# Projecting the first half of the even layer's heads from x without its shift, the shift's projection coming from two more columns of ctx's operand

## The chip, the cores and the metric

The kernel runs on one core of a Trainium2 chip. The metric is the device time of one execution in microseconds (us). Three runs of the kernel before gave a median of 1676.35 us (1673.29 to 1677.78).

## What is computed

Two layers of a transformer over x (512 rows of 1024) and a context ctx (256 rows of 1024), all in float32. The change lies at the very start of layer 0, the even layer:

```python
mod = silu_c @ ada_w[l] + ada_b[l]            # c gives x's six vectors
modc = silu_cc @ ada_w[l] + ada_b[l]          # c_ctx gives ctx's six
sh1, sc1, g1, sh2, sc2, g2 = split(mod, 6)    # 1024 each: shift, scale, gate, ...
a  = rmsnorm(h, norm1_g) * (1 + sc1) + sh1    # "modulate"
ac = rmsnorm(hc, norm1_g) * (1 + csc1) + csh1
...
u, v, q, k, vv = split(a @ w_in, ...)         # even_mixer
q, k = apply_rope(q, cos, sin), apply_rope(k, cos, sin)
...
y = concatenate([chunk_mlp(u, v), diff_out(o)]) @ w_out
```

`q` and `k` hold eight heads of 64, that is four pairs; ctx gets a q and a k as well, without rope. A projection is linear, so `(y + sh) @ W` is `y @ W` plus the row `sh @ W`, which is the same for all 512 rows of x.

## The kernel before

**Layout and precision.** Activations lie transposed: 1024 features as `KT` = 8 tiles of 128 partitions, rows along the free axis (`TX` = 512 for x, `TC` = 256 for ctx, `TA` = 768 together). Float32 precision is had by splitting each operand into a high half rounded to fp32r and the low rest: ScalarE casts the high half, VectorE or GpSimd subtracts it (`split`, lines 115 and 116; for a weight, lines 75 and 78 in `unit`). Each product then takes three matmuls, high by high, high by low, low by high (`mm3`, lines 99 to 101).

**Order.** The kernel is written as one program in the order of the mathematics, and a scheduler places each instruction on its engine by priority, which is the place in the program unless `tc.high_priority` raises it. Each engine then works through its list in order. `tc.issue_after(ins)` holds an instruction behind another one. An edit in one place can therefore change the lists far behind it too.

**The entry of `even`.** SyncE's queue loads x. `squares` and `rstd_diag` work out the norm of each row. The two vectors that layer 0 needs first, scale (`j` = 1) and shift (`j` = 0), are 1024 x 1024 products with c. `ada_load` brings a slab of `ada_w` (1 MB, two tiles of 128 rows, 4 buffers). `ada_step` (line 349) multiplies a tile of it, as the moving operand, with a 128x32 operand `cst` that holds silu(c) and silu(c_ctx): four matmuls, each into its own 32 rows of one PSUM tile `pf`. `ada_out` copies the result (line 356), transposes it (line 358) and adds the bias, for scale also the norm's gain (lines 362 and 366). There are two passes, scale first, then shift, and `warm` (line 374) puts matmuls without use between the steps. Between the passes VectorE multiplies the eight `hx` by scale and norm (line 392).

Then follows a loop over two halves of the heads. In each, for every `k`, a weight `qk[half, k]` (128 x 512, 256 KB) is loaded and split, x's operand `axx[k]` is made in the first half (line 455 adds the shift on ScalarE, line 456 makes the low half on VectorE), and `mm3` adds to four accumulators of 128 x 512 that fill both wide PSUM tiles (`pw`). In the middle of the first half come ctx's norm and, by `modulate` (lines 191 to 193), its operand `axc[k]`. The accumulators are copied out (`evacuate`), ctx is projected by the same weights into two single PSUM banks (`pb`), and x's part of q and k gets its rope. The operands of x and ctx are two slices, 512 and 256 columns, of one tile from a ring of 16 (`ax`). Between all these, `ada_some` puts in the steps for the other four vectors (two at a time, slabs of 128 x 2048).

**Behind the entry** come the V projection, the attention of four head pairs (`head`), the u and v projections and their gelu (`gated`, `gelu`), the norm of v (`turn`), the 128 x 128 mixing matmuls (`mix`, lines 649 and 650, on the one PSUM bank `fill`), the product u * v (line 677), and the splitting of all eight tiles into `cat`. The out projection (`project`) multiplies them with `even_out`, cast eight at a time by `slab`. `residual` (line 757) adds the result to the stream. None of these lines is touched by the change.

PSUM has two wide tiles (`pw`, two banks each), three single banks (`pb`) and one for small things (`pf`, `fill`).

Of the kernel before, what the change touches and what calls it, by code (L numbers as in the profile page):

```python
# [26 lines left out]
class Builder:  # L27
# [72 lines left out]
        mm(out, s[0], m[1], start=False, stop=False, **kw)  # L100
        mm(out, s[1], m[0], start=False, stop=stop, **kw)  # L101

    def ax(self):

        return [self.axp.tile([P, TA], F32R, name=self.uid("ax"), tag="ax", bufs=16) for _ in range(2)]
# [206 lines left out]
    def even(self):  # L312
# [24 lines left out]
        def ada_load(j, n, k):  # L337

            m = 2 // n
            t = self.adap.tile([P, m, n * D], F32, name=self.uid("ar"), tag="ar", bufs=4)  # L340
            src = a["ada0"][k * P:(k + m) * P, j * D:(j + n) * D].rearrange("(k p) c -> p k c", p=P)
            self.last_slab = nc.sync.dma_start(t, src)
            return [t[:, i, :] for i in range(m)]

        def ada_step(ps, k, t):

            w = t.shape[-1] // 4
            for q in range(4):
                nc.tensor.matmul(ps[32 * q:32 * q + 32, :w], cst[:, k, :], t[:, w * q:w * q + w], start=k == 0,
                                 stop=k == KT - 1, skip_group_check=True)  # L350

        def ada_out(j, n, ps, pt):

            row = self.tmp("t")
            nb = 2 * n
            nc.scalar.copy(row[:, :nb * P], ps[:, :nb * P])
# [24 lines left out]
        ps0 = self.fill()  # L381
        for k in range(KT):
            ada_step(ps0, k, slabs[k])
            if k % 2:
                slabs += ada_load(0, 1, k - 1)
# [4 lines left out]
        ada_out(1, 1, ps0, scaled)  # L390
        for k in range(KT):
            nc.vector.scalar_tensor_tensor(hx[k], hx[k], self.modcol(0, 1, k, 0), rx, ALU.mult, ALU.mult)
# [12 lines left out]
        loaded, ps_of = [], {}  # L405
# [12 lines left out]
                if k == KT - 1:  # L418
                    ada_out(j, 2, ps_of.pop(j), self.bank())

        hc = []
# [6 lines left out]
        tabs = []  # L428

        def evacuate(ps, n, c, heads):  # L430
            h = heads[n % 2]
# [2 lines left out]
                qk[key] = f3()  # L434
            nc.scalar.mul(qk[key][:, c], ps, 0.125 if n < 2 else 1.0)

        with tc.issue_after(self.last_slab.ins):
            ctx_load()
        for half, heads in enumerate(((0, 1), (2, 3))):
            w2 = [self.wide(), self.wide()]  # L440
            accx = [w[:, h * 512:(h + 1) * 512] for w in w2 for h in range(2)]
            W = []
            for k in range(KT):
                t = self.adap.tile([P, 2, 512], F32R, name=self.uid("wq"), tag="wq", bufs=3) if k % 3 == 2 else None
                with tc.issue_after(self.last_slab.ins) if half == 0 else ExitStack():
                    W.append(self.blocks(a["qk"][half, k], 512, t=t))
                    if half == 0:
                        if k > 4:
                            with tc.issue_after(self.last_w.ins):
                                ada_ahead(1)  # L450
                        if k == 7:
                            tabs += [self.load(self.ropep, a[n], [P, TX], n) for n in ("cos", "sin")]
                if half == 0:
                    t, sh = hx[k], self.modcol(0, 0, k, 0)
                    nc.scalar.activation(axx[k][0], t, AF.Identity, bias=sh)
                    nc.vector.scalar_tensor_tensor(axx[k][1], t, sh, axx[k][0].bitcast(F32), ALU.add, ALU.subtract)  # L456
                elif k % 2:
                    ada_ahead(1)
# [11 lines left out]
            bk = [self.bank() for _ in range(2)]  # L470
            accc = [b[:, h * TC:(h + 1) * TC] for b in bk for h in range(2)]
            for k in range(KT):
                for n in range(4):
                    self.mm3(accc[n], W[k][n], axc[k], k == 0 and n % 2 == 0, k == KT - 1)
                if k % 2 and k > 2 - half:
# [333 lines left out]
    def pair(self, pool):  # L809
        NH = self.T // 2  # L810
        if pool:
            t = pool.tile([P, 2, NH], F32R, name=self.uid("T"), tag="T", bufs=12)
            return t[:, 0, :], t[:, 1, :]
        t = self.axp.tile([P, TA], F32R, name=self.uid("ax"), tag="ax", bufs=16)
        return t[:, :NH], t[:, NH:2 * NH]

    def ffn_rstd(self, half, sq, rest, NH=TA // 2, bank=None):
# [259 lines left out]
    def odd(self):  # L1077
# [133 lines left out]
        raw = {}  # L1211

        def keep(half, n, eng):
            t = self.axp.tile([P, TA], F32R, name=self.uid("ax"), tag="ax", bufs=16)
# [128 lines left out]
```

## Time and profile before

| | |
|---|---|
| median of three runs | 1676.35 us |
| the profiled execution | 1676.23 us, its span 1674.4 us |
| TensorE busy | 1550.9 us (93%) |
| VectorE busy | 1152.9 us (69%) |
| ScalarE busy | 729.3 us (44%) |
| GpSimd busy | 658.4 us (39%) |
| DMA, mean over the span | 97 GB/s, 161.97 MB |

The span is the time from the first to the last recorded instruction. PE is TensorE's matmuls, PEld its weight loads, DVE VectorE, ACT ScalarE, POOL GpSimd, SP the queue of SyncE that issues the DMAs. In rows of the timeline the first two numbers are the start and the length of a group of instructions, both in us; what stands in brackets is the idle time ahead of it and what ended that. `mean` is TensorE's granted clock as a share of full speed. The profile divides the span in 40 slices of 41.9 us; the entry is the first three of them.

```profile
## 2 busy tenths in 40 slices
PE   6999989799889899999999988999986899999996
DVE  4622788855987889777766675665668866775675
DMA  8743000232032333444331112101140332323211
```

TensorE is busy for 9 tenths or more of most slices; the first slice, with 6 tenths, is one of the exceptions, and the eighth, where the out projection begins, is another with 7.

### The profile page before, as it was taken

How to read it: one execution, taken by the hardware profiler on the slowest of the kernel's cores; microseconds unless marked ns; L12 is line 12 of the kernel's file. 1: busy time of each engine (PE TensorE's matmuls, PEld its weight loads, DVE VectorE, ACT ScalarE, POOL GpSimd, SP SyncE). 2: the span in 40 equal slices, each digit the busy share in tenths (PEclk: the TensorE clock that was granted, in tenths of full speed). 3: DMA queues.
4: the chain of work that ended last, by engine and by line, in shares of the span. 5: the costliest groups of instructions: out<-in, count | busy, mean ns of one | idle time of the engine just before them, and what ended most of it. 6: DMA issues, size and time to landing. Idle time of an engine off the chain costs nothing.

```text
span 1674.4 us, 24582 instructions
## 1 busy us (share of the span) xinstructions
PE 1550.9 (93%) x9463; PEld 1358.2 (81%) x9463; DVE 1152.9 (69%) x2097; ACT 729.3 (44%) x1464; POOL 658.4 (39%) x477
## 2 busy tenths in 40 slices
PE   6999989799889899999999988999986899999996
PEld 4776878699689899999999877767776788888886
DVE  4622788855987889777766675665668866775675
ACT  2413676533532333333333334555555444444442
POOL 0463211231563433434343236422116755545562
PEclk9999989999899999999999989999998999999998
DMA  8743000232032333444331112101140332323211
GB/s 311 298 170 145 32 7 1 76 133 82 3 123 93 134 122 121 148 139 147 130 128 38 50 60 74 51 13 43 53 158 1 127 108 81 114 76 109 82 38 51
DMA packets 47957, 161.97 MB, mean 97 GB/s; under 512 B 5472, under 2 KB 9952, under 8 KB 40160
## 3 DMA queue, kind: packets, MB, share of 16 engines
q1 hardware_dynamic: 47696, 160.28, 27.0%
q8 instruction: 74, 1.21, 0.3%
q14 instruction: 43, 0.35, 0.1%
q10 hardware_dynamic: 144, 0.13, 0.0%
HBM read 158.29 MB, written 2.10 MB: 96 GB/s over the span
## 4 chain that ended last, share of the span: by engine, by line
PE 66%; DVE 16%; DMA 6%; issue 4%; ACT 4%; POOL 4%; POOLq 0%; SPq 0%; DVEq 0%; ACTq 0%
PE pw L99 8%; PE pb L99 8%; PE pw L100 7%; PE pb L100 7%; PE pw L101 7%; PE pb L101 7%; DMA raw<-ffn_in 4%; PE pf L99 3%; PE pf L100 2%; PE pf L101 2%; PE pb L1198 2%; PE pb L1192 2%; POOL w L903 2%; DVE t L925 2%; DVE junk L220 2%
## 5 line engine op out<-in xcount | busy, mean ns | idle before, releaser
L903 POOL TENSOR_TENSOR w<-raw,w 128x512 fp32r<-128x512 f32 x126 | 173.6, 1391 | 152.2 <-ACT w L901 146.0
L99 PE MATMUL pw<-ax,w 128*128 128x384 f32 (+2 forms) x640 | 209.0, 330 | 17.2 <-DVE hs L984 5.3
L78 POOL TENSOR_TENSOR w<-raw,w 128x512 fp32r<-128x512 f32 (+1 forms) x84 | 127.1, 1520 | 235.4 <-ACT w L75 213.4
L100 PE MATMUL pw<-ax,w 128*128 128x384 f32 (+2 forms) x640 | 208.1, 325 | 2.7 <-DVE ax L456 1.4
L101 PE MATMUL pw<-ax,w 128*128 128x384 f32 (+2 forms) x640 | 206.2, 325 | 1.3 <-POOL w L903 1.1
L903 POOL TENSOR_TENSOR w<-rawo,w 128x512 fp32r<-128x512 f32 x80 | 122.2, 1527 | 198.4 <-ACT w L901 192.2
L757 DVE SCALAR_TENSOR_TENSOR xT<-pb,mod,xT 128x512 f32<-128x512 f32 (+3 forms) x208 | 144.3, 703 | 48.2 <-PE pb L101 47.8
L99 PE MATMUL pw<-T,w 128*128 128x384 f32 (+1 forms) x504 | 159.0, 318 | 17.1 <-DVE hs L975 7.4
L99 PE MATMUL pb<-hh,w 128*128 128x512 f32 x480 | 166.5, 361 | 7.4 <-ACT hh L115 5.3
L100 PE MATMUL pb<-hh,w 128*128 128x512 f32 x480 | 171.2, 358 | 0.9 <-POOL hh L116 0.9
L101 PE MATMUL pb<-hh,w 128*128 128x512 f32 x480 | 168.8, 358 | 0.5 <-POOL w L903 0.5
L100 PE MATMUL pw<-T,w 128*128 128x384 f32 (+1 forms) x504 | 159.1, 316 | 3.5 <-POOL T L116 1.8
L101 PE MATMUL pw<-T,w 128*128 128x384 f32 (+1 forms) x504 | 158.3, 314 | 0.0
L99 PEld LDWEIGHTS pw<-ax,w 128*128 128x128 f32 x640 | 122.9, 193 | 32.5 <-DVE q L979 8.3
L901 ACT CAST w<-t 128x512 fp32r<-128x512 f32 x120 | 74.4, 621 | 151.3 <-DVE t L925 111.7
L100 PEld LDWEIGHTS pw<-ax,w 128*128 128x128 f32 x640 | 123.5, 193 | 10.1 <-DVE ax L193 2.7
L101 PEld LDWEIGHTS pw<-ax,w 128*128 128x128 f32 x640 | 123.3, 193 | 6.1 <-POOL w L903 2.6
L99 PEld LDWEIGHTS pw<-T,w 128*128 128x128 f32 x504 | 97.3, 194 | 23.6 <-ACT T L115 8.8
L116 POOL TENSOR_TENSOR hh<-hs,hh 128x768 fp32r<-128x768 f32 (+1 forms) x42 | 75.9, 1809 | 85.5 <-ACT hh L115 83.1
L99 PE MATMUL pb<-ax,w 128*128 128x256 f32 (+1 forms) x340 | 105.0, 311 | 3.0 <-ACT w L75 1.6
L903 DVE TENSOR_TENSOR w<-t,w 128x512 fp32r<-128x512 f32 x104 | 89.1, 857 | 24.4 <-ACT w L901 23.4
L99 PEld LDWEIGHTS pb<-hh,w 128*128 128x128 f32 x480 | 90.1, 190 | 18.8 <-ACT hh L115 6.0
(384 smaller groups left out, 4160.2 us busy)
## 6 DMA issues: line engine op xcount, KB each, us to landing
raw<-ffn_in SPq DMA_DIRECT2D x44, 1024.0 KB, 4.9
ar<-ada SPq DMA_DIRECT2D x24, 1024.0 KB, 6.7
ar<-ada SPq DMA_DIRECT2D x48, 512.0 KB, 3.5
rawo<-ffn_out SPq DMA_DIRECT2D x44, 512.0 KB, 3.6
raw<-odd_out SPq DMA_DIRECT2D x32, 256.0 KB, 2.6
raw<-qk SPq DMA_DIRECT2D x16, 256.0 KB, 7.7
raw<-uv SPq DMA_DIRECT2D x16, 256.0 KB, 2.7
raw<-even_out SPq DMA_DIRECT2D x8, 512.0 KB, 4.4
```

Source lines behind the costliest of these rows:

```text
L78: eng.tensor_tensor(lo, raw, hi.bitcast(F32), ALU.subtract)
L99: mm(out, s[0], m[0], start=start, stop=False, **kw)
L100: mm(out, s[0], m[1], start=False, stop=False, **kw)
L101: mm(out, s[1], m[0], start=False, stop=stop, **kw)
L116: return (lo_eng or nc.vector).tensor_tensor(lo, src, hi.bitcast(F32), ALU.subtract)
L220: self.nc.vector.scalar_tensor_tensor(junk, t, 1.0, self.cb[who], ALU.mult, ALU.mult, accum_out=self.acc[who][:, col:col + 1])
L757: self.nc.vector.scalar_tensor_tensor(h, ps[:, r], self.modcol(l, j, m, who), h, ALU.mult, ALU.add)
L901: nc.scalar.copy(t[:, 0, :], src)
L903: (eng or nc.gpsimd).tensor_tensor(t[:, 1, :], src, t[:, 0, :].bitcast(F32), ALU.subtract)
L925: nc.vector.tensor_tensor(t, x, y, how)
L1192: nc.tensor.transpose(pt[:, x * P:(x + 1) * P], es[2 * (x % 2) + x // 2][:, kb * P:(kb + 1) * P], self.ident)
L1198: nc.tensor.matmul(po[64 * h:64 * h + 64, :], V[vb][:, 64 * g:64 * g + 64], t[:, h * TC:h * TC + TC], start=kb == 0, stop=kb == nb - 1, sk ...
```

## The change

The pass for the shift no longer stands ahead of the first projection. The second `ada_load`, its eight steps and its 30 warm matmuls go; six warm matmuls stay behind the first pass. Line 392's scaling of `hx` moves into the loop of the first half, and its result is split as it is, without shift, by `split` (lines 118 and 119 now). After that loop `late` issues the shift's slabs, ctx and the rope tables behind the last weight, and a block with the priority of `k` = 2 makes ctx's norm, the eight steps for the shift, its transposes, and ctx's operand. `shift_parts` writes the shift, split in two, in two new columns behind ctx's 256 (tiles of 770 instead of 768 columns). The ctx projection of the first half works on 258 columns, in one wide tile and two banks; its column 256 is `sh @ W`, copied to a 128x1 `b` (line 500) and added to x's part of q or k (line 502). For the second half, and for the V, u and v projections behind it, x's operand is made anew with the shift (`shifted`, lines 429 and 430).

```diff
-        for k in range(KT):
-            nc.vector.scalar_tensor_tensor(hx[k], hx[k], self.modcol(0, 1, k, 0), rx, ALU.mult, ALU.mult)
-        ps0 = self.fill()
-        for k in range(KT):
-            ada_step(ps0, k, slabs[KT + k])
-            warm(slabs[KT + k][:, :P], 3)
-        row = ada_out(0, 1, ps0, scaled)
+        row = ada_out(1, 1, ps0, scaled)
         warm(row[:, :P], 6)
...
-        AX_ = [self.ax() for _ in range(KT)]
+        AX_ = [self.ax(2) for _ in range(KT)]
...
+        def shifted(out, t, sh):
+            nc.scalar.activation(out[0], t, AF.Identity, bias=sh)
+            nc.vector.scalar_tensor_tensor(out[1], t, sh, out[0].bitcast(F32), ALU.add, ALU.subtract)
+
+        def late():
+            with tc.issue_after(self.last_w.ins):
+                sl = sum([ada_load(0, 1, k) for k in range(0, KT, 2)], [])
+                ctx_load()
+            with tc.issue_after(self.last_slab.ins):
+                tabs.extend(self.load(self.ropep, a[n], [P, TX], n) for n in ("cos", "sin"))
+            return sl
+
+        def shift_parts():
+            for k in range(KT):
+                sh = self.modcol(0, 0, k, 0)
+                hi, lo = [t[:, TA:TA + 2] for t in AX_[k]]
+                nc.vector.tensor_copy(hi, sh.to_broadcast([P, 2]))
+                nc.vector.tensor_tensor(lo, sh.to_broadcast([P, 2]), hi.bitcast(F32), ALU.subtract)
...
                 if half == 0:
-                    t, sh = hx[k], self.modcol(0, 0, k, 0)
-                    nc.scalar.activation(axx[k][0], t, AF.Identity, bias=sh)
-                    nc.vector.scalar_tensor_tensor(axx[k][1], t, sh, axx[k][0].bitcast(F32), ALU.add, ALU.subtract)
-                elif k % 2:
-                    ada_ahead(1)
-                    ada_some()
+                    t = hx[k]
+                    nc.vector.scalar_tensor_tensor(t, t, self.modcol(0, 1, k, 0), rx, ALU.mult, ALU.mult)
+                    self.split(*axx[k], t)
+                else:
+                    shifted(axx[k], hx[k], self.modcol(0, 0, k, 0))
+                    if k % 2:
+                        ada_ahead(1)
+                        ada_some()
                 for n in range(4):
                     self.mm3(accx[n], W[k][n], axx[k], k == 0, k == KT - 1)
-                if half == 0 and k == 4:
+                if half == 0 and k == 2:
+                    here = tc.cur_priority
+            if half == 0:
+                sl = late()
+                with tc.high_priority(offset=tc.cur_priority - here):
                     rd = self.rstd_diag([(self.squares(hc, TC), TC)], 1.0 / D)[0]
-                if half == 0 and k == 5:
+                    ps0 = self.fill()
+                    for k in range(KT):
+                        ada_step(ps0, k, sl[k])
+                    ada_out(0, 1, ps0, scaled)
                     rc = self.spread(rd)
+                    shift_parts()
                     for i in range(KT):
                         self.modulate(hc[i], TC, self.modcol(0, 1, i, 1), self.modcol(0, 0, i, 1), rc, axc[i])
...
             for n in range(4):
-                evacuate(accc[n], n, slice(TX, TA), heads)
+                evacuate(bk[n][:, :TC], n, slice(TX, TA), heads)
+                if half == 0:
+                    b = self.small(1, "qb", 4)
+                    nc.scalar.mul(b, bk[n][:, TC:TC + 1], 0.125 if n < 2 else 1.0)
+                    q = qk[n if n < 2 else 2 + n][:, :TX]
+                    nc.scalar.activation(q, q, AF.Identity, bias=b)
```

The lists of the engines below show what the scheduler makes of it. Each row names the line, the operation, its output and inputs, the shape, and how often it stands in a row; the line numbers of the changed kernel are larger (349 is 352 there, 149 is 152, 115 is 118, 205 is 208, 622 is 645, 649 is 672).

VectorE at the entry, before: behind the scaling of `hx` (line 392) come ctx's squares (line 185) and the shift's bias (line 362), then the first low half of x (line 456).

```order
L392 SCALAR_TENSOR_TENSOR hx_5_93<-hx_5_93,mod_66,pb_190 128x512 x2
L392 SCALAR_TENSOR_TENSOR hx_6_95<-hx_6_95,mod_66,pb_190 128x512 x2
L185 TENSOR_TENSOR sq_425<-sq_425,q_427 128x256
L185 TENSOR_TENSOR sq_425<-sq_425,t_430 128x256
L362 TENSOR_TENSOR mod_66<-pb_222,adab_135 128x8
L362 TENSOR_TENSOR mod_67<-pb_222,adab_135 128x8
L185 TENSOR_TENSOR sq_425<-sq_425,q_433 128x256
L185 TENSOR_TENSOR sq_425<-sq_425,t_436 128x256
L185 TENSOR_TENSOR sq_425<-sq_425,q_439 128x256
L456 SCALAR_TENSOR_TENSOR ax_309<-hx_3_89,mod_66,ax_308 128x512
```

The same place after; `subg` is a 128x1 constant of the attention.

```order
L457 SCALAR_TENSOR_TENSOR hx_3_89<-hx_3_89,mod_66,pb_186 128x512 x2
L457 SCALAR_TENSOR_TENSOR hx_4_91<-hx_4_91,mod_66,pb_186 128x512 x2
L457 SCALAR_TENSOR_TENSOR hx_5_93<-hx_5_93,mod_66,pb_186 128x512 x2
L457 SCALAR_TENSOR_TENSOR hx_6_95<-hx_6_95,mod_66,pb_186 128x512 x2
L538 TENSOR_SCALAR subg_1332<-subg_1332 128x1
L119 TENSOR_TENSOR ax_230<-hx_3_89,ax_229 128x512
L119 TENSOR_TENSOR ax_232<-hx_3_89,ax_231 128x512
L119 TENSOR_TENSOR ax_234<-hx_4_91,ax_233 128x512
```

All eight scalings still stand together ahead of the first low half, although the program now has them one by one in the loop; the ctx squares and the shift's bias come later.

ScalarE at the entry, after; `raw` is a weight as loaded, `pf_163` the scale's product.

```order
L75 CAST w_249<-raw_247 128x512
L75 CAST w_269<-raw_267 128x512
L359 COPY t_215<-pf_163 128x256
L75 CAST wq_287<-raw_288 128x512
L75 CAST w_309<-raw_307 128x512
L75 CAST w_329<-raw_327 128x512
L118 CAST ax_229<-hx_3_89 128x512
L75 CAST wq_347<-raw_348 128x512
```

Two weights are cast ahead of the copy of the scale's product, the others behind it.

TensorE at the entry, before: the shift's steps (`ar` is a slab) alternate with warm matmuls, ahead of the first projection.

```order
L358 MATMUL pb_222<-ident_97,t_223 128x128 x2
L349 MATMUL pf_239<-ar_174,cst 32x256 x4
L374 MATMUL pw_103<-ar_174,ones 128x128 x3
L349 MATMUL pf_239<-ar_174,cst 32x256 x4
L374 MATMUL pw_103<-ar_174,ones 128x128 x3
L349 MATMUL pf_239<-ar_188,cst 32x256 x4
```

After, they stand between the projections of the fifth and the seventh of the first half's eight weights (`pw` from `ax` and `wq`, here the sixth):

```order
L352 MATMUL pf_466<-ar_409,cst 32x256 x4
L99 MATMUL pw_245<-ax_239,wq_347 128x512
L352 MATMUL pf_466<-ar_409,cst 32x256
L100 MATMUL pw_245<-ax_240,wq_347 128x512
L352 MATMUL pf_466<-ar_409,cst 32x256
L152 MATMUL pb_447<-ones,sq_423 128x128 x2
L352 MATMUL pf_466<-ar_409,cst 32x256
L101 MATMUL pw_245<-ax_239,wq_347 128x512
L352 MATMUL pf_466<-ar_409,cst 32x256
L99 MATMUL pw_245<-ax_239,wq_347 128x512
L352 MATMUL pf_466<-ar_411,cst 32x256
L100 MATMUL pw_245<-ax_240,wq_347 128x512
```

A step's four matmuls no longer stand in a row there: matmuls of the projection stand between them one at a time.

TensorE where the out projection begins, before: `f` is v's normed tile, `w_3256` the first weight of `even_out`, line 175 the last norm of the attention.

```order
L649 MATMUL pf_3129<-sguT_1295,f_353_1910 128x128 x4
L649 MATMUL pf_3139<-sguT_1295,f_353_1910 128x128 x2
L649 MATMUL pf_3145<-sguT_1295,f_360_1973 128x128 x4
L99 MATMUL pw_3312<-ax_3193,w_3256 128x384
L100 MATMUL pw_3312<-ax_3194,w_3256 128x384
L99 MATMUL pw_3313<-ax_3193,w_3256 128x384
L100 MATMUL pw_3313<-ax_3194,w_3256 128x384
L175 MATMUL pb_2769<-q_2761,ones 128x512
```

After:

```order
L672 MATMUL pf_3166<-sguT_1316,f_365_1994 128x128 x4
L178 MATMUL pb_2790<-q_2782,ones 128x512
L178 MATMUL pb_2793<-q_2787,ones 128x256
L672 MATMUL pf_3176<-sguT_1316,f_365_1994 128x128 x2
L672 MATMUL pf_3182<-sguT_1316,f_372_2057 128x128 x4
L672 MATMUL pf_3192<-sguT_1316,f_372_2057 128x128 x2
L672 MATMUL pf_3198<-sguT_1316,f_379_2120 128x128 x4
L672 MATMUL pf_3208<-sguT_1316,f_379_2120 128x128 x2
L99 MATMUL pw_3333<-ax_3214,w_3277 128x384
```

All mixing now stands ahead of the first matmul of the projection.

ScalarE at the same place, before; `cb` are the copies of c that the next stage needs, `f_554` a tile of u * v.

```order
L622 ACTIVATE f_581_3062<-f_581_3062 128x768
L75 CAST w_3256<-raw_3257 128x1024
L75 CAST w_3255<-raw_3261 128x1024
L115 CAST ax_3207<-f_554_2807 128x768
L205 ACT_TABLE_LOAD
L205 ACTIVATE cb_3265<-cb_3265 128x1024
```

After:

```order
L208 ACTIVATE cb_3289<-cb_3289 128x1024
L118 CAST ax_3228<-f_559_2828 128x768
L118 CAST ax_3234<-f_568_2913 128x768
L118 CAST ax_3240<-f_577_2998 128x768
L118 CAST ax_3246<-f_586_3083 128x768
L118 CAST ax_3250<-o_2477 128x768
L75 CAST w_3277<-raw_3278 128x1024
L75 CAST w_3276<-raw_3282 128x1024
```

The first weights of the out projection are now cast behind the four products and the last tile of the attention.

More of the change, by code (lines that the diff above doesn't have):

```diff
@@ L101, in mm3, with ax, ax_tile @@
         mm(out, s[1], m[0], start=False, stop=stop, **kw)
-    def ax(self):
-        return [self.axp.tile([P, TA], F32R, name=self.uid("ax"), tag="ax", bufs=16) for _ in range(2)]
+    def ax(self, extra=0):
+        return [self.ax_tile()[:, :TA + extra] for _ in range(2)]
+    def ax_tile(self):
+        return self.axp.tile([P, TA + 2], F32R, name=self.uid("ax"), tag="ax", bufs=16)
     def small(self, cols, tag="sm", bufs=6):
@@ L383, in even @@
             ada_step(ps0, k, slabs[k])
-            if k % 2:
-                slabs += ada_load(0, 1, k - 1)
             if k == 3:
@@ L419, in ada_some @@
                     ada_out(j, 2, ps_of.pop(j), self.bank())
-        hc = []
+        hc, tabs = [], []
         def ctx_load():
@@ L426, in ctx_load @@
                 hc.extend(t[:, n, :] for n in range(4))
-        tabs = []
         def evacuate(ps, n, c, heads):
@@ L469, in even @@
                 evacuate(accx[n], n, slice(0, TX), heads)
-            bk = [self.bank() for _ in range(2)]
-            accc = [b[:, h * TC:(h + 1) * TC] for b in bk for h in range(2)]
+            if half == 0:
+                extra = 2
+                w = self.wide()
+                bk = [w[:, :TC + 2], w[:, TX:TX + TC + 2]] + [self.bank()[:, :TC + 2] for _ in range(2)]
+            else:
+                extra = 0
+                bk = [b[:, h * TC:(h + 1) * TC] for b in [self.bank() for _ in range(2)] for h in range(2)]
             for k in range(KT):
                 for n in range(4):
-                    self.mm3(accc[n], W[k][n], axc[k], k == 0 and n % 2 == 0, k == KT - 1)
-                if k % 2 and k > 2 - half:
+                    self.mm3(bk[n], W[k][n], [t[:, TX:TA + extra] for t in AX_[k]], k == 0 and (half == 0 or n % 2 == 0),
+                             k == KT - 1)
+                if k % 2 and (half or k > 3):
                     ada_ahead(1)
@@ L478, in even @@
             for n in range(4):
-                evacuate(accc[n], n, slice(TX, TA), heads)
+                evacuate(bk[n][:, :TC], n, slice(TX, TA), heads)
+                if half == 0:
+                    b = self.small(1, "qb", 4)
+                    nc.scalar.mul(b, bk[n][:, TC:TC + 1], 0.125 if n < 2 else 1.0)
+                    q = qk[n if n < 2 else 2 + n][:, :TX]
+                    nc.scalar.activation(q, q, AF.Identity, bias=b)
             for h in heads:
@@ L813, in pair @@
             return t[:, 0, :], t[:, 1, :]
-        t = self.axp.tile([P, TA], F32R, name=self.uid("ax"), tag="ax", bufs=16)
+        t = self.ax_tile()
         return t[:, :NH], t[:, NH:2 * NH]
@@ L1213, in keep @@
         def keep(half, n, eng):
-            t = self.axp.tile([P, TA], F32R, name=self.uid("ax"), tag="ax", bufs=16)
+            t = self.ax_tile()
             t = t[:, :TC], t[:, TC:TX]
```

9 lines of the change are left out of this document (removed).

## The prediction

> **What bounds it now.** Times below are microseconds from the start of the profiled execution. I read the windows first, then TensorE's timeline, then VectorE, GpSimd and the DMA issues around each of TensorE's gaps. Columns of the windows: length, busy time of PE, PEld, DVE, ACT, POOL, granted clock, DMA share, GB/s.
>
> ```profile
> span 1674.4 us, 24582 instructions
> 40.16:61.19 21.03, 19.36 (x81) 13.84 (x82) 14.68 (x21) 8.17 (x15) 11.46 (x8) 1.00 0.90 331
> 61.19:123.27 62.08, 62.08 (x396) 47.81 (x394) 24.26 (x50) 20.86 (x42) 37.29 (x27) 1.00 0.53 189
> 200.00:300.00 100.00, 88.00 (x546) 76.82 (x547) 85.87 (x218) 69.34 (x144) 12.32 (x8) 0.95 0.01 4
> 320.00:340.00 20.00, 12.12 (x70) 10.72 (x69) 19.06 (x43) 8.81 (x11) 8.73 (x4) 0.74 0.42 133
> 340.00:373.00 33.00, 33.00 (x200) 32.90 (x199) 14.11 (x14) 10.54 (x12) 16.31 (x6) 1.00 0.31 109
> ```
>
> From 61.19 to 123.27 TensorE has no gap (62.08 of 62.08): in the entry every microsecond that work is added to TensorE, or that it starts later, is a microsecond of the kernel. From 320 to 340 it is idle for 7.9 us behind VectorE (19.06 of 20 busy); then it is full again. DMA moves 1 to 4% between 200 and 300, so no backlog of transfers waits there that a delay could hide under. The two places that the change reorders are thus worth their own time.
>
> **The entry: when does TensorE start?** Before, the first projection matmul stands at 40.16, behind the second pass over `ada`:
>
> ```profile
> 25.84 0.37 ACT L356 COPY t<-pf 128x256 f32<-128x256 f32 x1 [15.45 <-PE pf L349]
> 27.14 5.36 DVE L392 SCALAR_TENSOR_TENSOR hx<-hx,mod,pb 128x512 f32<-128x512 f32 x8
> 40.16 0.73 PE L99 MATMUL pw<-ax,w 128*128 128x512 f32 x2 [0.42 <-ACT ax L455]
> ar<-ada SPq DMA_DIRECT2D x1, 1024.0 KB, 14.3
> 46.34 1.07 DVE L128 TENSOR_SCALAR sm<-sm 128x2 int32<-128x2 int32 x1
> 47.32 1.87 DVE L456 SCALAR_TENSOR_TENSOR ax<-hx,mod,ax 128x512 fp32r<-128x512 f32 x1
> 50.48 0.74 DVE L456 SCALAR_TENSOR_TENSOR ax<-hx,mod,ax 128x512 fp32r<-128x512 f32 x1
> 47.34 1.30 POOL L78 TENSOR_TENSOR wq<-raw,wq 128x512 fp32r<-128x512 f32 x1
> 48.61 1.74 POOL L78 TENSOR_TENSOR w<-raw,w 128x512 fp32r<-128x512 f32 x1
> L757 DVE SCALAR_TENSOR_TENSOR xT<-pb,mod,xT x208: 337/740/752, 375.5 to 1658.8; 128x512 f32<-128x512 f32 x88, 128x256 f32<-128x256 f32 x12, 128x384 f32<-128x384 f32 x2, 128x128 f32<-128x128 f32 x2
> ```
>
> The last slab of the first pass is issued at 5.4 and takes 14.3, so it lands at 19.7; the weights now queue right behind it and no longer bind. ScalarE's order puts the third weight's cast behind the copy that ends at 26.2, so GpSimd gets weights three to eight from 26.8 on: six at 1.30 end at 34.6. VectorE meanwhile scales all eight `hx` first: these read one operand from PSUM, and of 208 such operations beside a working GpSimd none took over 752 ns, so 27.14 + 5.36 = 32.5 stands. Then come `subg` and the low half of x, with both operands in SBUF, and these do wait: L128, tiny, lasts 1.07 to the end of a GpSimd operation, and the L456 right behind it loses 1.87 to the next one (0.74 alone). So `subg` waits for the GpSimd operation that ends at 33.3, the first low half for the one that ends at 34.6, and is there at **35.2**. TensorE has run two matmuls by then and stands. Bounds: 33.9 if only one such wait is met, 36 if GpSimd is slowed as in its 1.74. The Trainium skill's "SBUF — State Buffer" (the box of ports) says that whichever of the two starts first holds the shared ports for its whole instruction and the other fully blocks. By that alone VectorE could go first after the one wait, and the start and the sum would be 1.0 lower; the pair L128, L456 lost two turns in a row, so I keep 35.2.
>
> TensorE has then stood for 6 us. What that does to its speed, and what the moved `ada` matmuls cost:
>
> ```profile
> 11.91 2.05 PE L149 MATMUL pb<-ones,sq 128*128 128x128 f32 x8 [11.91 <-DVE sq L185]
> 18.22 0.64 PE L349 MATMUL pf<-ar,cst 128*32 128x256 f32 x8
> 18.79 0.71 PE L374 MATMUL pw<-ar,ones 128*128 128x128 f32 x4
> 1302.09 0.58 PE L99 MATMUL pw<-ax,w 128*128 128x256 f32 x1 [3.17 <-ACT hs L968]
> 1302.46 0.41 PE L100 MATMUL pw<-ax,w 128*128 128x256 f32 x1
> 1305.14 0.28 PE L101 MATMUL pw<-ax,w 128*128 128x256 f32 x1
> 51.92 0.40 PE L99 MATMUL pw<-ax,w 128*128 128x512 f32 x1
> 52.24 1.05 PE L349 MATMUL pf<-ar,cst 128*32 128x512 f32 x4
> 53.23 0.50 PE L100 MATMUL pw<-ax,w 128*128 128x512 f32 x1
> 53.57 0.40 PE L101 MATMUL pw<-ax,w 128*128 128x512 f32 x1
> 53.81 0.40 PE L99 MATMUL pw<-ax,w 128*128 128x512 f32 x1
> 90.66 1.06 PE L349 MATMUL pf<-ar,cst 128*32 128x512 f32 x8
> 62.17 3.63 PE L349 MATMUL pf<-ar,cst 128*32 128x512 f32 x28
> 66.07 0.27 PE L100 MATMUL pb<-ax,w 128*128 128x256 f32 x1
> 62.87 0.88 DVE L193 SCALAR_TENSOR_TENSOR ax<-t,mod,ax 128x256 fp32r<-128x256 f32 x2 [0.18 <-ACT ax L192]
> ```
>
> After 3.17 us of waiting the matmuls run slow from 1302.09 until 1305; at the very start they are slow from 11.91 to 18.22. Half of that is lost: 1.4 to 3.1; I take 2.0. The Trainium skill's "TensorE: Matmul & The Clock Gate" (Part 1) gives about 3.4 us of half rate after an idle window, so 1.7.
>
> The `ada` step costs by group, not by matmul. Two matmuls of 512 columns between projections (x4, two records each) hold TensorE from 52.24 to 53.23; four (x8, at 90.66) last the same 1.06; fourteen in one run take 3.63, four rounds of 0.9. Around a group 0.09 is lost ahead and 0.11 behind (53.23 to 53.57 is 0.34, a matmul 0.23). Four of 256 columns take 18.22 to 18.79 = 0.57. One alone among projections I therefore price at half of 0.9, 0.43, plus the 0.33 of changing over and back: 0.76; bounds 0.14 (a fourth of 0.57, nothing for changing) and 1.0 (the 512 row). In the new order 14 of the 32 stand alone and the others in runs of 5, 6 and 7, two rounds each, 1.2: 14 x 0.76 + 3 x 1.2 = **14.2**. Before, all 32 lay ahead of 40.16. Their cover, `ada` slabs still landing, is gone.
>
> Sum for the entry, at the point where the second half's ctx projection ends (123.27 before):
> - start 35.2 instead of 40.16: -5.0
> - waits of before between 40.16 and 61.19 not repeated (21.03, less 72 matmuls at 0.228, one step of 1.2 and statistics of 0.5): -2.9
> - two matmuls run ahead: -0.5
> - slow TensorE: +2.0
> - `ada` matmuls: +14.2; the two transposes of their result: +0.7
> - ctx: its low halves wait behind VectorE's rewriting of the second half's x. From the shift columns on, 16 tiny operations (2 us), then eight L456 of 0.74 and the L191 and L193 (0.44) mixed among them; the first is hidden by the 16 later `ada` matmuls (3.75), the second comes 1.7 late: +1.7 (0 to 3.5)
> - 512-column `ada` steps in fewer groups: -1.2; two columns on 96 matmuls of 0.12: +0.1
>
> That is **+9.1** (lowest terms -3.5, or +6 with the small matmuls at 0.6; highest +15). The biases (eight short ScalarE operations) and the wide PSUM tile that ctx takes cost nothing: twenty matmuls of the second half stand ahead of the first one that needs that tile. The warm matmuls removed were waiting time. SP's moved loads (slabs, ctx, tables) have 20 us to land.
>
> **The out projection.** The new order also changes what stands at 320 to 373, though no line there is touched:
>
> ```profile
> 325.62 1.80 DVE L128 TENSOR_SCALAR sm<-sm 128x6 int32<-128x6 int32 x1
> 329.11 4.64 POOL L78 TENSOR_TENSOR w<-raw,w 128x1024 fp32r<-128x1024 f32 x2
> 333.70 0.68 DVE L650 TENSOR_TENSOR f<-pf,sgub 128x512 f32<-128x512 f32 x1
> 327.10 1.98 ACT L75 CAST w<-raw 128x1024 fp32r<-128x1024 f32 x2
> 334.43 1.22 PE L649 MATMUL pf<-sguT,f 128*128 128x128 f32 x4 [6.91 <-DVE f L650]
> 336.17 2.08 PE L649 MATMUL pf<-sguT,f 128*128 128x128 f32 x8 [0.52 <-DVE f L650]
> 336.15 0.96 DVE L677 TENSOR_TENSOR f<-f,f 128x768 f32<-128x768 f32 x1
> 337.90 0.67 PE L99 MATMUL pw<-ax,w 128*128 128x384 f32 x1
> 373.41 2.19 DVE L757 SCALAR_TENSOR_TENSOR xT<-pw,mod,xT 128x384 f32<-128x384 f32 x4 [6.03 <-PE pw L101]
> ```
>
> Before, two weights are cast at 327.10, projection starts at 337.90, and the other mixes are done between its matmuls; it ends at 373.4. After, ScalarE casts no weight of it until all mixes, products and casts are done. One gain: GpSimd is free from 329.1, the small VectorE operations stop waiting, and L650 comes at 329.6 instead of 333.70. But then the four mix rounds run alone on one PSUM bank: round one 2.4, round two with the norm 5.6, two more at 3.1 to 4.4 (matmuls at full or at the half rate of 334.43 and 336.17, L650 of 0.68 and 0.42), the last product 1.0: 344.8 to 347.4. Two casts of 0.8 and the weight's 1.0 follow: TensorE starts at about 348.8, 1.0 slow, and needs 35.5 less the 2.3 of mixes and norms: 383.0 against 373.4, **+9.6** (8 to 11).
>
> The attention order between 200 and 315 also changes: 12 us of idle TensorE there could become 7 or 17; I take 0 and keep 5 either way in the range. Total +18.7 on the profiled 1676.23 (span 1674.4 and 1.8 around it; the median of three is 1676.35): **1695**.
>
> **Rivals.**
> - The entry alone loses; the later order evens out. For: that order is full of such exchanges. Against: the casts stand where they stand. 1685, chance 0.13.
> - The lone `ada` matmuls cost their streaming share, 32 x 0.14 = 4.6: entry -0.5, out projection as above, 1685, 0.12. With both, 1676 and no change: 0.12.
> - The start gains nothing: every low half waits for GpSimd, or weights come late, and TensorE starts at 40: 1700, 0.05. Against it: GpSimd has nothing left after 34.6.
> - Faster: the new order of 200 to 375 fills TensorE's gaps instead of adding to them. There is 12.0 + 7.9 idle, and 1 between 300 and 320; it decides from 14 of these 21 recovered (9.1 + 5). At 17: 1668, 0.08. For it: whole gated blocks move between attention steps. Against it: VectorE is busy for 85.87 of 100 there.
>
> **How the numbers follow.** The forecast has 0.50. Slower holds 0.50 + 0.13 + 0.12 + 0.05 = 0.80, no change 0.12, faster 0.08 (0.3% is 5 us, about what three runs can tell). The terms' own bounds give 1688 to 1704 for the forecast; to hold 8 in 10 the range goes down past the two 1685 cases: 1681 to 1704.
>
> **What would show it.** First full run of projections near 35, after a gap from 29; lone small matmuls at 0.7 to 0.8; the V projection starting near 132 instead of 123; weight casts of the out projection after 355 on the shifted clock, TensorE with no projection for some 25 us. Wrong if a lone `ada` matmul costs 0.15, if the entry ends by 126, or if the out projection ends less than 12 later than before.

## The result, and the profile after

The changed kernel takes 1687.6 us (five runs, 1684.6 to 1691.31) beside 1677.78 us for the kernel before: a ratio of 1.0062 [1.0041, 1.0084]. In a second session (the first experiment below) it took 1691.32 beside 1678.06, 1.0072 [1.0054, 1.0089]. Slower was forecast, at 1695 in 1681 to 1704. The profiled execution is the slowest of its five, 1691.31 us with a span of 1689.5, so stages are compared here by landmarks, and the end by the medians.

The timeline of TensorE after, at the landmarks that the prediction used (start, length, then what it is; the wait ahead in brackets):

```profile
29.11 0.73 PE L99 MATMUL pw<-ax,w 128*128 128x512 f32 x2 [1.55 <-ACT ax L118]
34.37 0.79 PE L100 MATMUL pw<-ax,w 128*128 128x512 f32 x1 [4.53 <-DVE ax L119]
34.96 0.63 PE L101 MATMUL pw<-ax,w 128*128 128x512 f32 x1
...
130.07 0.50 PE L99 MATMUL pw<-w,ax 128*128 128x512 f32 x1
...
351.56 0.71 PE L672 MATMUL pf<-sguT,f 128*128 128x128 f32 x4 [0.78 <-DVE f L673]
356.41 0.69 PE L99 MATMUL pw<-ax,w 128*128 128x384 f32 x1 [4.14 <-ACT w L75]
```

Two matmuls run at 29, the first low half lets TensorE go on at 34.37, the V projection starts at 130.07 (123.27 before), and the out projection starts at 356.41 behind a wait of 4.14 for ScalarE's cast of its weight. The stages as windows, from the V projection to the first mixing matmul, to the out projection's start, to its first residual, and about 100 us on; first the changed kernel, then the kernel before:

```profile
130.07:336.00 205.93, 190.69 (x1108) 157.59 (x1104) 139.93 (x351) 116.01 (x228) 35.07 (x24) 0.97 0.15 54
336.00:356.41 20.41, 10.27 (x53) 7.88 (x53) 18.40 (x35) 9.18 (x11) 2.77 (x2) 0.87 0.05 19
356.41:390.92 34.51, 34.51 (x184) 34.51 (x185) 0.12 (x1) 7.09 (x7) 18.94 (x8) 0.93 0.58 217
390.92:488.50 97.58, 84.54 (x405) 73.39 (x404) 76.95 (x143) 44.91 (x99) 37.03 (x27) 0.95 0.12 45
```

```profile
123.27:326.37 203.10, 188.74 (x1109) 156.53 (x1105) 138.76 (x351) 116.47 (x228) 35.69 (x25) 0.97 0.15 56
326.37:337.90 11.53, 4.11 (x20) 3.62 (x21) 10.64 (x17) 3.46 (x4) 7.38 (x4) 0.60 0.31 91
337.90:373.41 35.51, 35.51 (x210) 34.98 (x210) 16.16 (x19) 12.61 (x14) 16.31 (x6) 0.98 0.30 106
373.41:473.10 99.69, 86.75 (x414) 76.66 (x413) 76.23 (x144) 45.19 (x99) 37.34 (x27) 0.90 0.22 80
```

The entry loses 6.8, attention 2.8 (205.93 against 203.10). In the mixing VectorE is busy for 18.40 of 20.41 us, and it lasts 8.9 longer; the projection behind it is 1.0 shorter. At the first residual the kernel is 17.5 late, and the 100 us behind that give back 2.1. (The first residual is the third row's end: 390.92 in the changed kernel, 373.41 in the one before.)

The first pass over `ada` ends at a different time from one execution to the next, between 25.3 and 26.8 in the profiles of this document, also where the entry's code is the same. Its end is taken as VectorE's first operation on its result, here before and after:

```profile
26.74 0.24 DVE L362 TENSOR_TENSOR mod<-pb,adab 128x8 f32<-128x8 f32 x2 [6.36 <-PE pb L358]
26.26 0.24 DVE L365 TENSOR_TENSOR mod<-pb,adab 128x8 f32<-128x8 f32 x2 [8.95 <-PE pb L361]
```

From there to the V projection it is 96.5 us in all three profiles with the old entry (before, and b_late and b_gate1 below) and 103.8 to 104.0 in the three with the changed one (after, a_again, e_cast). So the entry itself loses 7.3 to 7.5; the 6.8 also contains a first pass that happened to end 0.5 sooner.

### The profile page after: what moved, and what is told of

Its sections match the earlier page's. It is cut to its first block, busy times and chain, and to the rows that moved or that the text cites. A ratio compares the mean times of both kernels' runs of the same rounds, so it can differ in the third digit from the quotient of the medians.

```text
span 1689.5 us, 24536 instructions
## 1 busy us (share of the span) xinstructions
PE 1555.7 (92%) x9415; PEld 1354.4 (80%) x9415; DVE 1145.7 (68%) x2121; ACT 736.4 (44%) x1480; POOL 658.2 (39%) x477
## 3 DMA queue, kind: packets, MB, share of 16 engines
q1 hardware_dynamic: 47696, 160.28, 26.8%
## 4 chain that ended last, share of the span: by engine, by line
PE 69%; DVE 15%; DMA 5%; ACT 4%; issue 3%; POOL 3%; SPq 0%; POOLq 0%; ACTq 0%; DVEq 0%
PE pw L99 9%; PE pw L100 8%; PE pw L101 8%; PE pb L99 8%; PE pb L100 8%; PE pb L101 8%; DMA raw<-ffn_in 3%; PE pf L99 3%; PE pf L100 2%; PE pf L101 2%; PE pb L1221 2%; PE pb L1215 2%; DVE t L948 2%; DVE w L926 2%; DVE junk L223 2%
## 5 line engine op out<-in xcount | busy, mean ns | idle before, releaser
L99 PE MATMUL pw<-ax,w 128*128 128x384 f32 (+3 forms) x652 | 212.8, 329 | 24.9 <-DVE hs L1007 7.2
L100 PE MATMUL pw<-ax,w 128*128 128x384 f32 (+3 forms) x652 | 211.7, 325 | 6.1 <-DVE ax L119 4.5
L101 PE MATMUL pw<-ax,w 128*128 128x384 f32 (+3 forms) x652 | 208.8, 324 | 1.5 <-POOL w L926 1.4
L99 PEld LDWEIGHTS pw<-ax,w 128*128 128x128 f32 x652 | 124.6, 192 | 40.9 <-DVE hs L1007 8.5
L100 PEld LDWEIGHTS pw<-ax,w 128*128 128x128 f32 x652 | 125.3, 192 | 12.9 <-DVE ax L119 5.0
L101 PEld LDWEIGHTS pw<-ax,w 128*128 128x128 f32 x652 | 125.1, 192 | 7.2 <-POOL w L926 3.0
L75 ACT CAST w<-raw 128x512 fp32r<-128x512 f32 (+1 forms) x100 | 64.5, 653 | 98.5 <-PE pb L101 40.4
L99 PE MATMUL pb<-ax,w 128*128 128x256 f32 (+2 forms) x328 | 102.6, 315 | 3.2 <-ACT w L75 2.0
```

Of the source, the lines that this page charges most:

```text
L75: nc.scalar.copy(hi, raw)
L99: mm(out, s[0], m[0], start=start, stop=False, **kw)
```

## The experiments

**The same kernel again** (a_again).

> The changed kernel once more, for a second profile. If the shifts of the first profile belong to the change, they come back: the V projection starts near 130.1 (6.8 later than before), the first mixing matmul stands near 336.0 (+9.6), the first residual of the out projection near 390.9 (+17.5), each within 1 us, and the time is 1684 to 1691. If they are the luck of one execution, at least one of the first three moves by 2 us or more. What lies behind 391 us is read from the same profile: I expect +10 to +17 at the end, since the second half of the kernel waits for its weights' loads.

| landmark, us | before | after | again |
|---|---|---|---|
| end of the first `ada` pass | 26.74 | 26.26 | 26.31 |
| V projection | 123.27 | 130.07 | 130.27 |
| first mixing matmul | 326.37 | 336.00 | 336.39 |
| first residual | 373.41 | 390.92 | 391.40 |
| span | 1674.4 | 1689.5 | 1687.7 |

Up to the first residual the shifts belong to the change: they come back within 0.5. At the span's end they are +15.1 and +13.3.

**The ada matmuls in one run** (e_group): `last_mm` is the last matmul that `mm3` issued.

```diff
+                if half == 0 and k == 5:
+                    hold = self.last_mm
...
+                    with tc.issue_after(hold.ins):
                         for k in range(KT):
                             ada_step(ps0, k, sl[k])
```

> The changed kernel with the shift's 32 ada matmuls held behind the last projection matmul of the sixth weight, so that 30 of them stand in one run. Theory A, a lone ada matmul between projections costs 0.75 us because of the change over and back: 30 in one run take 4 to 5 us and the two lone ones 1.5, against 13.7 now, so the V projection starts near 122 instead of 130.1 and the time is about 1679.5 (8 less than the changed kernel). Rival B, the lone matmuls only fill time in which TensorE would wait for weights, slabs or ctx: the V projection starts at 128 or later and the time stays at 1686 or more.

TensorE's timeline in the changed kernel, among its lone matmuls:

```profile
52.24 0.50 PE L99 MATMUL pw<-ax,wq 128*128 128x512 f32 x1
52.67 0.62 PE L352 MATMUL pf<-ar,cst 128*32 128x256 f32 x2
53.22 0.50 PE L100 MATMUL pw<-ax,wq 128*128 128x512 f32 x1
...
56.38 0.51 PE L99 MATMUL pw<-ax,wq 128*128 128x512 f32 x1
56.82 0.62 PE L352 MATMUL pf<-ar,cst 128*32 128x256 f32 x2
57.37 0.50 PE L100 MATMUL pw<-ax,wq 128*128 128x512 f32 x1
```

and in the grouped one:

```profile
53.81 3.22 PE L352 MATMUL pf<-ar,cst 128*32 128x256 f32 x52
56.95 0.49 PE L99 MATMUL pw<-ax,w 128*128 128x512 f32 x1
57.38 0.62 PE L352 MATMUL pf<-ar,cst 128*32 128x256 f32 x2
57.93 0.49 PE L100 MATMUL pw<-ax,w 128*128 128x512 f32 x1
```

With two records for each matmul, a lone one between two projection matmuls takes them from 52.24 to 53.22, 0.98 apart instead of 0.23: 0.75. Twenty-six in a run last from 53.81 to 56.95, 0.12 each. (Four more stand in a run ahead of it, and two stay alone.) The V projection starts at 123.09, 7.0 to 7.2 earlier, and the time is 1683.98 (ratio to before 1.0032 [1.0018, 1.0046]), 7.3 below the changed kernel of the same session. Theory A holds; the missing 1 us of its 8 is a new wait of 1.35 for a weight's cast.

**VectorE's order at the entry** (e_inter): `los` holds the low halves.

```diff
-                    nc.vector.scalar_tensor_tensor(t, t, self.modcol(0, 1, k, 0), rx, ALU.mult, ALU.mult)
-                    self.split(*axx[k], t)
+                    with tc.issue_after(los[k - 2].ins) if k > 1 else ExitStack():
+                        nc.vector.scalar_tensor_tensor(t, t, self.modcol(0, 1, k, 0), rx, ALU.mult, ALU.mult)
+                    los.append(self.split(*axx[k], t))
```

> The changed kernel with VectorE's order at the entry made scale, scale, split, scale, split ... instead of eight scalings and then eight low halves. Theory A, the first projection waits for VectorE's order alone: the first low half starts near 29.1, waits for GpSimd's operation that ends near 30.1 and is there at 30.8; the first high-by-low matmul moves from 34.4 to 30.8, the V projection from 130.1 to 126.6, the time to about 1684. Rival B, the low halves wait for all of GpSimd's weight work, which ends at 33.8: the start stays at 34 and the time at 1687.6. Rival C: the start moves, and the weights or slabs then come late and give it back: the V projection stays above 129.

The first high-by-low matmul came at 29.80, 4.6 earlier; 0.9 of that is this execution's earlier first pass (its end at 25.37), and the other 3.7 are what A said. But the V projection came only 1.9 sooner, at 128.16 (1.0 to 1.2 counted from the first pass), and the time is 1688.79 (1.0062 [1.0041, 1.0083]). So A holds for the start and not for the V projection. C has the direction, but neither its 129 nor its cause: 18 instead of 14 ada matmuls stand alone in the new order, and TensorE waits 2.3 for ctx's operand.

**The out projection's order on the kernel before** (b_late): `last_hi` is the last cast of a product.

```diff
-        slab(0)
-        slab(1)
+        with tc.issue_after(self.last_hi.ins):
+            slab(0)
+            slab(1)
```

> The kernel before with its entry untouched, and ScalarE's casts of the out projection's first two weights put behind the last cast of the products, which gives TensorE and ScalarE the order that the changed kernel has there. Theory A, this order alone makes the out projection late: the stretch from the first mixing matmul to the first residual grows from 47.0 to 54.9 us, and the time rises by 7.8 to about 1685.5. Rival B, the out projection of the changed kernel is late because of what reaches it late from the attention: the stretch grows by 3 us at most and the time by less than 3.

The stretch from the first mixing matmul to the first residual became 57.04 (47.04 before, 54.92 and 55.01 in the changed kernel), the time 1688.77 (1.0049 [1.0032, 1.0066]). Rival B falls: with the entry untouched, this order alone makes the stretch 10 us longer. It is 2 more than in the changed kernel, and 1.5 of that comes from VectorE's list: here a product's low half (line 116, at 342.71) stands ahead of the fourth tile's `L650` (343.59), and the mixing matmuls wait 2.29 for it, where the changed kernel has the two the other way round and waits 0.78.

**The casts first, in the changed kernel** (e_cast): an edge puts the first product's cast behind the two weights' casts.

```diff
+        tc.add_manual_dep(first.ins, self.last_cast.ins.name, ...)
```

> The changed kernel with ScalarE's casts of the out projection's first two weights put ahead of the cast of the first product; TensorE still has all mixing matmuls first. Theory A, of the 7.9 us that the out projection loses, 4.1 are the wait for those casts behind the last mixing matmul (4.14 us of idle TensorE in the profile) and the other 3.8 are the mixing standing alone: the first projection matmul moves from 356.4 to 352.3, the stretch from the first mixing matmul to the first residual from 54.9 to 50.8, the time by -4. Rival B, the weights' buffers are not free until the mixing is done, so an earlier place in the list buys nothing: the stretch stays above 54. Rival C, the early casts hold up the products' casts and so the later weights' matmuls: the start moves, the first residual does not.

None of the three holds. The casts ran early, at 340.28, so B's buffers were free, though the stretch did stay above its 54: it grew to 58.14 and the time to 1697.54 (1.0110 [1.0094, 1.0127]). VectorE's timeline, GpSimd's, and TensorE's waits in this kernel:

```profile
341.17 0.15 DVE L134 SCALAR_TENSOR_TENSOR sm<-sm,sm 128x6 f32<-128x6 f32 x1
342.17 2.31 DVE L135 SCALAR_TENSOR_TENSOR sm<-sm,sm 128x6 f32<-128x6 f32 x1
344.51 5.40 DVE L168 TENSOR_SCALAR q<-ident,sm 128x128 f32<-128x128 f32 x6
```

```profile
341.38 7.67 POOL L78 TENSOR_TENSOR w<-raw,w 128x1024 fp32r<-128x1024 f32 x3 [2.38 <-ACT w L75]
```

```profile
PE pb L178 <- DVE q L168: 6.2, 1, 6.2
```

The earlier casts released GpSimd's low halves into VectorE's norm: an operation of 0.17 took 2.31, six of 1.27 together took 5.40, and TensorE waited 6.2 for them. In the changed kernel GpSimd is idle there. After that wait the granted clock was 0.50 until the projection began (349.58 to 362.21; 0.92 from 343.06 to 352.27 in the changed kernel): eight records of mixing matmuls took 2.08 instead of 1.16, which is part of the loss too.

**TensorE kept busy** (e_warm): `warm(row[:, :P], 32)` instead of 6.

> The changed kernel with 32 instead of 6 matmuls without use behind the first ada pass, which keep TensorE busy to about 32.5 while it waits for the first low half. Theory A, the first matmuls behind the wait are slow because TensorE stood idle before: they come every 0.23 us instead of 0.43, and the V projection starts 1.2 us earlier, near 128.9. Rival B, they are slow for another reason (operands arriving, GpSimd's port): 0.43 stays, and the V projection starts at 130.1. The sum in the prediction had 2.0 us for this.

The matmuls from 33.85 on came 0.23 apart, and the granted clock from 34 to 40 was 1.00 instead of 0.73: theory A. The V projection started at 128.76, 1.3 to 1.5 earlier, but 0.6 of that is the first pass, which ended at 25.69. The slow matmuls themselves cost 1.1: from the first low half to the first ada matmul TensorE takes 3.20 here (33.85 to 37.05) and 4.30 in the changed kernel (34.37 to 38.67). The whole time (1692.44, two runs) doesn't resolve that.

**Both entry edits** (e_gi), and **all three** (e_gic).

> The changed kernel with both edits at the entry: the ada matmuls in one run behind the sixth weight, and VectorE's scalings and low halves in turn. If the two losses are separate, their gains add up: first high-by-low matmul at 29.8, the V projection near 118.5 (130.1 less 7.0 less 4.6), the time 6 below that of the grouped kernel alone less what attention does. If the entry then meets its next limit, the second half's weights (1.3 us of wait for a weight's cast were already there in the grouped kernel) or ctx, the V projection starts at 120 to 123. I expect 120.5 and about 1681.

> All three edits: grouped ada matmuls, VectorE's order at the entry, the two weights' casts ahead of the products' casts. If each works as alone, it is 4 us below the kernel with the two entry edits, near 1677, so level with the kernel before; if the cast edit buys nothing, near 1681.

With both entry edits the V projection started at 117.64, and the time is 1678.2 beside 1679.72 (0.9985 [0.9972, 0.9999]): level with the kernel before. The four other profiles with this entry (e_gic and the three behind it) show 120.1 to 120.7, and 120.5 was expected. The 117.64 is luck of that execution: its first pass ended 1.0 to 1.5 sooner, and its granted clock from 28 to 34 was 1.00, where the four have 0.72 to 0.81 (e_inter had the same luck with its clock). Counted from the end of the first pass, the four reach the V projection after 93.8 to 94.0, the old entry after 96.5: with both edits the changed entry gains 2.6 instead of losing. With the casts first as well: 1688.09, since those work as in e_cast (stretch 58.04), not as expected.

**GpSimd held back** (e_gate2): on top of e_gic, `gate` is a 128x1 operation that reads the third mixed tile.

```diff
+                gate = nc.gpsimd.tensor_tensor(self.small(1), raw[6][:, 512:513], raw[6][:, 512:513], ALU.add)
...
+        with tc.issue_after(gate.ins):
+            slab(0)
+            slab(1)
```

> The kernel with both entry edits, and the weights' casts put first as in e_cast, but GpSimd's low halves of those two weights held until the third mixed tile is done (a 128x1 operation on GpSimd that reads it). Theory A, e_cast lost because GpSimd's three weight operations (7.67 us) blocked VectorE's small operations, and the early casts themselves are a gain: TensorE's first projection matmul comes right behind the last mixing matmul, the stretch from the first mixing matmul to the first residual falls from 54.9 (e_gi) to about 50.8, the time by 4 to about 1674. Rival B, the casts themselves hold up what VectorE and TensorE wait for: the stretch stays at 55 or above.

The stretch fell to 49.59 and the time to 1673.48 beside 1678.93 (0.9967 [0.9955, 0.9979]). So GpSimd was what made the early casts a loss.

**GpSimd's two low halves to VectorE** (e_vec), and **both** (e_gv3, gate behind the last mixed tile).

> The kernel with both entry edits, and the low halves of the two attention tiles that GpSimd makes (4.1 us, beside VectorE's norm) made by VectorE instead; casts as in the changed kernel. Theory A, GpSimd's two operations hold VectorE's tiny operations (1.80 and 1.72 instead of 0.17 each), which delays the mixing by 3.2, while the two low halves cost VectorE 1.9: the stretch falls by 1.3 to 53.6. Rival B, VectorE's added 1.9 is all that shows: 56 to 57.

> Both of these edits together, GpSimd's low halves of the weights held until the last mixed tile is done. If the two gains add, the stretch is about 49.5 and the time about 1673, which is 0.3% below the kernel before; if the low halves now come too late for TensorE, the start of the projection moves to about 340 and the first residual does not.

Alone, with the casts as in the changed kernel, the stretch is 52.66 (2.3 less than in e_gi; 1.3 expected). With the casts first and the gate it is 48.51. The times are 1679.07 (1.0002 [0.9988, 1.0016]) and 1673.94 (0.9973 [0.9959, 0.9986]). The first gain does not show in the time; in the second kernel TensorE waits 2.58 for a weight's low half, which takes back part of what the start gained, and the time is no better than e_gate2's.

**The same gate in the kernel before** (b_gate1), behind the first part of the second mixed tile.

> The kernel before, its entry untouched, with GpSimd's low halves of the out projection's first weights held until the first part of the second mixed tile is done (a 128x1 operation on GpSimd that reads it); the casts stay where they are. Theory A, GpSimd blocks VectorE's small operations in the kernel before too: two of them last 2.26 us beside GpSimd's 4.64, and the mixing matmuls wait 6.91 us behind them. Without that the first residual comes 2.5 us earlier (the wait shrinks by 4, and TensorE then waits 1.5 for the weight's low half): the stretch from the first mixing matmul to the first residual falls from 47.0 to about 44.5, the time by 2.5. Rival B, the low halves come too late instead: the stretch stays at 47 or grows.

It is the fastest kernel here: 1670.51 beside 1679.18, 0.9950 [0.9934, 0.9965]. The stretch is 43.82, 3.2 less (2.5 expected). VectorE's timeline before, which goes on with the prediction's `L650` at 333.70:

```profile
329.21 2.26 DVE L131 SCALAR_TENSOR_TENSOR sm<-sm,sm 128x6 f32<-128x6 f32 x1
331.51 2.26 DVE L132 SCALAR_TENSOR_TENSOR sm<-sm,sm 128x6 f32<-128x6 f32 x1
```

and VectorE's and TensorE's with the gate:

```profile
328.89 0.17 DVE L131 SCALAR_TENSOR_TENSOR sm<-sm,sm 128x6 f32<-128x6 f32 x1
329.09 0.17 DVE L132 SCALAR_TENSOR_TENSOR sm<-sm,sm 128x6 f32<-128x6 f32 x1
329.18 0.69 DVE L650 TENSOR_TENSOR f<-pf,sgub 128x512 f32<-128x512 f32 x1
```

```profile
329.92 1.22 PE L649 MATMUL pf<-sguT,f 128*128 128x128 f32 x4 [2.74 <-DVE f L650]
```

The wait fell from 6.91 to 2.74: theory A. The time fell by more than that explains. The first residual is 3.6 earlier than in the profile of before and the end of the span 8.3, so the larger part of the gain lies far behind the edit, and its cause stays open. A kernel in which TensorE's projection matmuls stand between the mixing ones again, with the changed entry, was not run.

## Why the prediction was right, and where its sizes were off

- **The start: right, 0.8 early.** 35.2 was said for the first low half, 34.37 measured. Of GpSimd's six weights the first began at 26.32 and the last ended at 33.77 (26.8 and 34.6 said), and that is the 0.8; 0.5 of it comes from the earlier end of the first pass. `subg` (0.15) did not wait for GpSimd; the low half did, for that last weight, as said:

```profile
32.93 0.15 DVE L538 TENSOR_SCALAR subg<-subg 128x1 f32<-128x1 f32 x1
32.99 3.13 DVE L119 TENSOR_TENSOR ax<-hx,ax 128x512 fp32r<-128x512 f32 x4
```

  Four last 3.13 and the later ones 0.68 each, so the first had one wait. Nothing of GpSimd's stood behind that weight, so these rows can't say whether VectorE would have lost a second turn. In e_inter one stands behind it: there the first low half took 1.54 (one wait) and GpSimd's next operation 1.75 instead of 1.27. The Trainium skill's "SBUF — State Buffer" (Who interferes with whom) has the engine that comes second wait for one whole instruction: e_inter agrees.
- **Slow TensorE: right, over-sized.** 2.0 was said; e_warm shows 1.1. The estimate from the figure of the Trainium skill's "TensorE: Matmul & The Clock Gate" (Part 1), 1.7, is nearer, and too high as well.
- **The lone ada matmuls: right.** 0.76 each was said, 0.75 measured. Of the 16.91 us from 50.27 to 67.18, sixteen projection matmuls are 3.7 and two for ctx's norm 0.6; with the other group at 38.67 the whole term is near 13.7 (14.2 said). e_group shows it by taking 7 away, and the rival with 0.14 each falls.
- **ctx's low halves, +1.7: wrong.** No such wait is in the changed kernel; a slab of `ada` came 0.9 late instead. In e_gi, where the entry is faster, ctx's operand is waited for by 2.3.
- **The entry's sum:** 9.1 said, 6.8 and 7.0 measured at the V projection, 7.3 to 7.5 counted from the end of the first pass. The four points above come to 3.0 (0.8, 0.9, 0.5, and the 1.7 less the slab's 0.9), more than the difference of 2.1 to 2.3; the rest is not accounted for.
- **Attention, 0 within 5: inside.** +2.8 and +3.0 against the profile of before. The stretch is 205.9 to 206.7 in every kernel with the changed entry, and 203.1 to 204.1 in the three with the old one, so the loss is some 2 to 3. About 0.5 lies in the V projection (41.33 instead of 40.80); which reorder behind it costs the rest stays open. The 0 was the middle of a range, not a reading.
- **The out projection: right, 1.7 too high.** +9.6 was said, +7.9 measured, and b_late shows that the order alone does it. The mixing ended 17.8 us behind its first matmul (18.4 to 21 said), since most of TensorE's small matmuls were not at half rate; behind it came the casts, as said.
- **What lies behind: the step that failed.** The sum was carried to the end as it stood. At the first residual it was nearly right (17.5 and 18.0, 18.7 said), partly by luck: the entry and the out projection were 2.3 and 1.7 too high, and the 2.8 of attention, set at 0, made up for most of it. The next 100 us gave back 2.1 in the changed kernel and in its repeat, and 1.7 to 2.2 in e_group, e_inter and b_late. That seems to go with the order of the casts rather than with being late: e_cast and e_gic, where the weights are cast first, took 99.8 and 99.7 there and gave back nothing (99.7 before), though e_cast is the latest of all at the first residual, at 394.37. From there to the end the profiles differ by up to 10 us (1195.4 to 1205.6), so the rest of the way from 18 to the 10 and 13 us of the medians is not settled.

The rival with a start at 40 falls by 34.37; the rival in which attention and the out projection refill TensorE falls by +2.8 and +7.9.

## What to carry to other kernels

Price narrow matmuls by how often they alternate with wide ones: one narrow matmul between wide ones cost as much as six in a run, and grouping the same 32 gave back 7 us. An earlier cast is worth nothing if it releases another engine's work into the critical chain, so look at who is set free by a move, and hold that work with a tiny dependent operation. When an edit reorders code that it doesn't touch, put that order alone on the old kernel: it was the largest of this loss's three parts (7.9 of 17.5 us), and holding GpSimd back, found on the way, made the old kernel faster too. Before you read a difference of 1 us between two landmarks, see whether something ahead of both edits ended at another time.

## What the hardware showed that was not expected

Beside a running GpSimd operation of two inputs, VectorE's smallest operations with inputs in SBUF took 1.7 to 2.3 us instead of 0.17, yet the 128x1 `subg` took 0.15. It goes both ways: in e_inter, where VectorE's low halves stand between, the timeline of GpSimd shows two operations of 3.45 where two take 2.52 alone:

```profile
26.68 2.52 POOL L78 TENSOR_TENSOR w<-raw,w 128x512 fp32r<-128x512 f32 x2
29.15 1.75 POOL L78 TENSOR_TENSOR wq<-raw,wq 128x512 fp32r<-128x512 f32 x1
30.85 3.45 POOL L78 TENSOR_TENSOR w<-raw,w 128x512 fp32r<-128x512 f32 x2
```
